# A two-layer encoder step on one core: when loaded operands are cast, and in which order a lone block's seven products run

## The chip, the cores and the metric

The kernel runs on one core of a Trainium2 chip. The metric is the device time of one execution in microseconds (us), the median of several runs. TensorE (PE) does the matrix products, VectorE (DVE), ScalarE (ACT) and GpSimd (POOL) the rest; SyncE (SP) issues most of the loads and stores. Each engine takes its instructions in the order in which they stand in its queue.

## The reference

Two residual layers work on 1088 rows of 1024 features (1024 prompt frames, 64 frames of a running stream). Layer 0 mixes by a state-space scan, layer 1 by attention over a band of chunks; each is followed by a feed-forward part (FFN). The change lies in the FFN's first product, `u @ w_in`, and in the handing over to the second:

```python
def swiglu(u, w_in, w_out):
    g, up = jnp.split(u @ w_in, 2, axis=-1)
    return (jax.nn.silu(g) * up) @ w_out

def reference(...):
    for layer in range(DEPTH):
        ...                         # mixer or attention, with its norms
        xp = xp + rmsnorm(swiglu(rmsnorm(xp, nw[2]), ffn_w_in[layer], ffn_w_out[layer]), nw[3])
        xs = xs + rmsnorm(swiglu(rmsnorm(xs, nw[2]), ffn_w_in[layer], ffn_w_out[layer]), nw[3])
```

The hidden width is 2816: 22 tiles of 128 columns for the gate g and 22 for up.

## The kernel before

**Split operands.** Every float32 operand is used as a sum of two parts that TensorE takes at full speed: a high part, cast on ACT (L365 for weights, L1182 for activations, L1682 and L1710 for what is loaded for the second product), and a low part, the difference to it (L366, L1183, L1683, L1711, on DVE, and on POOL for one weight half). A product of two such operands is three matrix products: hi by hi, hi by lo, lo by hi (L1477 to L1479).

**Seven products for eight.** The rows are cut in halves, and so are the 1024 features. For a gate tile and its up tile together, the two by two blocks are multiplied with seven products P1 to P7 instead of eight, each of 12 matrix products (4 blocks of features by 3). The row operands a11, a21, ..., and their sums s1 to s4, are made once a layer by `op_build` for two row blocks, b=0 (256 columns a product) and b=1 (288). The weight operands are made for every pair of tiles t by `Weights.pair`: "ta" and "tb" are each two differences (L323, L324, on POOL, and L341, L342, on DVE), "r0" is a plain half and "b22" a quarter with its own small buffer `half`. Each is split as above.

**One pair of tiles, `run_pair`.** P1, P6 and P7 add up in one PSUM bank, A: after each, ACT copies the partial sum out (L1490, into p1, u2, u3), and the next may only then add on. P5 and P3 share a bank B where a pair runs for both row blocks. DVE adds the other products to the copies (L1492, L1495, L1498, L1500, L1506), ACT takes Silu (L1493, L1501), DVE multiplies gate and up (L1503, L1508). The order of the products is a list:

```python
PRODS = [
    (P1, "r0", 0, 0), (P2, "r0", 512, 2), (P6, "ta", 0, 1), (P5, "tb", 0, 3),
    (P7, "ta", 512, 5), (P4, "tb", 512, 6), (P3, "b22", 0, 4),
]
```

A pair runs for both row blocks in turn at each product, so that b=0's product lies between b=1's product and the copy of it. Some pairs have no such partner. `RUN` lists the pairs of a layer: in layer 0 t=5 to 21 for both blocks, and then t=0 to 4 for b=1 alone (for b=0 these five tiles are done earlier, without the seven products, by `plain_pairs`); in layer 1 t=5, then t=4 alone, then 6 to 21, then 0 to 3 alone. The first pair of each layer (t=5) is `apart`: all seven products of b=0, then all of b=1, because the splits of b=1 are not made yet. "Lone" below means a pair of b=1 alone.

**Loaders.** The gated results go to DRAM and come back as operands of the second product W2. From the end of t=21 a loader runs beside the lone pairs (`loader` in layer 0, `loader7` in layer 1): it loads a tile into a staging buffer `sg` (five of them), ACT casts it, DVE takes the low part. In layer 1 DVE also forms sums of the results for W2 (`Hidden.form`, L1396) and SP stores them.

**What sets the order.** PE's order is that of the program, with other tasks woven in by a planner (`Stream`) that yields at given times. On ACT, DVE, POOL and SP a scheduler places each instruction by priority (`HIP` for a pair's results, `LDP` for the loaders) and by when its operands are expected.

## Time and profile before

| | |
|---|---|
| median of 3 runs | 3064.5 us (3063.54 to 3070.5) |
| profiled execution | 3060.02 us, of it 3058.1 us span and 1.9 us around it |
| PE, busy | 2949.2 us, 96% of the span |
| DVE | 2228.4 us, 73% |
| ACT | 1478.1 us, 48% |
| POOL | 677.7 us, 22% |
| mean granted clock of PE | 0.988 of full speed |

Times in the rows below are counted from the start of the span. Layer 0's first products with seven instead of eight run from about 940 to 1374 us, the lone pairs from 1312 on; layer 1's from about 2370 to 2806 us, the lone pairs from 2752 on. In a row of the timeline the first two numbers are start and length in us, and the brackets give the idle time of the engine before it and the instruction that ended it. A "waits" row reads: who waited for whom, total us, how often, the longest.

### The profile page before, as it was taken

What the parts mean: (1) busy time and instruction counts of PE and PEld (TensorE: products, weight loads), DVE (VectorE), ACT (ScalarE), POOL (GpSimd) and SP (SyncE); (2) the same over time, 40 slices, a digit from 0 to 9 for tenths busy, and PEclk for the clock granted to TensorE, in tenths of its full rate; (3) what the DMA queues carried; (4) which work ended last, traced back from release to release, by engine and by line L of the source; (5) the groups of instructions that cost most, each with busy time, mean ns of one, the idle gap of its engine ahead of it and who ended that gap; (6) DMA issues with size and microseconds to landing.
All of it is one profiled execution on the core that took longest, in us unless ns stands there. A gap on an engine that the chain in (4) does not pass through costs nothing. (4 is left out here: it accounts for less than half of the span.)

```text
span 3058.1 us, 58284 instructions
## 1 busy us (share of the span) xinstructions
PE 2949.2 (96%) x22017; PEld 2883.2 (94%) x22017; DVE 2228.4 (73%) x4869; ACT 1478.1 (48%) x2834; POOL 677.7 (22%) x809
## 2 busy tenths in 40 slices
PE   8999999999999999989999999999899999999998
PEld 8899999999999999989999898999899999999998
DVE  8988888885878666683666777777668766667567
ACT  6655656554444333353444655555544433344552
POOL 1333333421342221220222000000053221211011
PEclk9999999999999999999999999999999999999999
DMA  3333333335443544445654212222344333235665
GB/s 118 115 91 105 93 102 96 102 111 166 153 138 109 158 133 149 158 146 170 209 177 146 82 62 87 62 62 76 116 140 132 106 108 117 92 120 178 184 193 185
DMA packets 244842, 385.69 MB, mean 126 GB/s; under 512 B 25584, under 2 KB 197168, under 8 KB 244560
## 3 DMA queue, kind: packets, MB, share of 16 engines
q1 hardware_dynamic: 244496, 381.89, 39.8%
q8 instruction: 173, 2.83, 0.4%
q14 instruction: 109, 0.89, 0.1%
q0 software_dynamic: 64, 0.07, 0.0%
HBM read 293.54 MB, written 83.86 MB: 123 GB/s over the span
## 5 line engine op out<-in xcount | busy, mean ns | idle before, releaser
L486 PE MATMUL mm<-r,hl 128*128 128x384 f32 (+2 forms) x1632 | 548.3, 336 | 6.8 <-ACT r L2161 6.0
L488 PE MATMUL mm<-r,hl 128*128 128x384 f32 (+2 forms) x1632 | 530.2, 325 | 3.6 <-DVE hl L378 2.7
L487 PE MATMUL mm<-r,hl 128*128 128x384 f32 (+2 forms) x1632 | 529.4, 324 | 0.7 <-DVE r L2162 0.7
L366 DVE TENSOR_TENSOR hl<-raw,hl 128x1024 fp32r<-128x1024 f32 (+1 forms) x245 | 288.0, 1176 | 200.5 <-ACT hl L365 193.8
L1478 PE MATMUL px<-r,hl 128*128 128x288 f32 (+1 forms) x1192 | 351.4, 295 | 0.0
L365 ACT CAST hl<-raw 128x1024 fp32r<-128x1024 f32 (+1 forms) x245 | 240.8, 983 | 191.1 <-PE po L1854 51.0
L1477 PE MATMUL px<-r,hl 128*128 128x288 f32 x1056 | 312.9, 296 | 13.8 <-ACT u L1490 8.3
L486 PEld LDWEIGHTS mm<-r,hl 128*128 128x128 f32 x1632 | 311.1, 191 | 8.7 <-ACT r L2161 6.2
L488 PEld LDWEIGHTS mm<-r,hl 128*128 128x128 f32 x1632 | 310.3, 190 | 5.3 <-DVE hl L378 4.2
L487 PEld LDWEIGHTS mm<-r,hl 128*128 128x128 f32 x1632 | 311.1, 191 | 1.4 <-DVE r L2162 1.0
L1479 PE MATMUL px<-r,hl 128*128 128x288 f32 x1056 | 311.8, 295 | 0.0
L512 POOL TENSOR_TENSOR ssum<-ssum,sq 128x256 f32<-128x256 f32 (+3 forms) x146 | 157.6, 1082 | 526.2 <-ACT sq L511 512.3
L1477 PE MATMUL px<-rx,hl 128*128 128x256 f32 x816 | 231.0, 283 | 9.6 <-ACT p L1490 9.6
L1479 PE MATMUL px<-rx,hl 128*128 128x256 f32 x816 | 229.9, 282 | 0.5 <-DVE hl L366 0.5
L1478 PEld LDWEIGHTS px<-r,hl 128*128 128x128 f32 x1192 | 225.8, 189 | 0.0
L1477 PEld LDWEIGHTS px<-r,hl 128*128 128x128 f32 x1056 | 199.7, 189 | 15.7 <-ACT u L1490 9.7
L1479 PEld LDWEIGHTS px<-r,hl 128*128 128x128 f32 x1056 | 199.4, 189 | 0.0
L1478 PE MATMUL px<-rx,hl 128*128 128x256 f32 x680 | 191.1, 281 | 0.0
L323 POOL TENSOR_TENSOR tt<-raw 128x512 f32<-128x512 f32 x44 | 61.5, 1398 | 584.1 <-DVE hl L366 513.3
L1490 ACT COPY u<-px 128x288 f32<-128x288 f32 (+1 forms) x156 | 60.1, 386 | 224.0 <-PE px L1479 209.2
L1477 PEld LDWEIGHTS px<-rx,hl 128*128 128x128 f32 x816 | 156.3, 192 | 10.3 <-ACT p L1490 10.3
L1479 PEld LDWEIGHTS px<-rx,hl 128*128 128x128 f32 x816 | 156.2, 191 | 0.8 <-DVE hl L366 0.8
(420 smaller groups left out, 8595.0 us busy)
## 6 DMA issues: line engine op xcount, KB each, us to landing
raw<-in_w_f_dram SPq DMA_DIRECT2D x156, 512.0 KB, 3.8
raw<-in_w_in_dram SPq DMA_DIRECT2D x40, 512.0 KB, 3.5
raw<-in_w_so_dram SPq DMA_DIRECT2D x32, 512.0 KB, 3.8
raw<-in_w_f_dram SPq DMA_DIRECT2D x33, 384.0 KB, 3.2
dm<-acd SPq DMA_DIRECT2D x64, 192.0 KB, 3.6
sg<-hop SPq DMA_DIRECT2D x77, 144.0 KB, 3.0
sg<-hop SPq DMA_DIRECT2D x83, 128.0 KB, 3.1
sg<-in_w_f_dram SPq DMA_DIRECT2D x48, 192.0 KB, 3.1
```

What stands on the lines that cost most here:

```text
L323: g(ta[:, 512:], b22, b12, op=ALU.subtract)
L365: self.nc.scalar.copy(h, v)
L366: (eng or self.eng or self.nc.vector).tensor_tensor(lo, v, h, op=ALU.subtract)
L486: PE.matmul(ps[:, :n], h_, xh, start=(first and i == 0), stop=False)
L487: PE.matmul(ps[:, :n], h_, xl, start=False, stop=False)
L488: PE.matmul(ps[:, :n], l_, xh, start=False, stop=(last and i == nk - 1))
L512: (eng or G).tensor_tensor(ssum[:, :n], ssum[:, :n], q[:, :n], op=ALU.add)
L1477: PE.matmul(ps, wh, ah[:, k, :], start=(k == 0 and not on), stop=False, skip_group_check=on)
L1478: PE.matmul(ps, wh, al[:, k, :], start=False, stop=False, skip_group_check=on)
L1479: PE.matmul(ps, wl, ah[:, k, :], start=False, stop=(k == 3), skip_group_check=on)
L1490: A.copy(x[nm_], ps)
```

## The change

Six edits, all in what surrounds the first product:

1. Pairs that are lone or apart use another order of products, `SINGLE`: P1, P3, P6, P2, P7, P5, P4. Here P3 gets its own bank (C), and P2 and P4 another (D); u2 takes C after P6 and B after P5, c22 is made after P5, and both multiplies come with P4.
2. In `op_build` for b=1 the sums come in the order s3, s2, s4, s1, and the splits in the order in which `SINGLE` uses them.
3. For the pair after the first and for lone pairs ("dve") the differences of L323 and L324 and the low part of b22 are made on VectorE, not on GpSimd.
4. The cast of b22 is gated in every pair: a one-column copy on POOL into its buffer reads the last pair's `ta`, so that the cast cannot come before that is made.
5. The loaders' casts are no longer issued with their loads. `late_cast` holds them back until two later loads are issued, and gates each by a one-column copy on POOL from `hid.gate`, the result that ACT copied out last. The loads get a planned pause (`LGAP`: 1.5 us in layer 0, 0.5 in layer 1).
6. `form` writes s2 into a tile of its own ("ssum", three buffers), and its groups are gated by `hid.gate`.

```diff
+LAHEAD, LGAP = 2, (1.5, 0.5)
...
     def pair(self, it):
-            g = self.nc.gpsimd.tensor_tensor
+            g = (self.nc.vector if "dve" in it else self.nc.gpsimd).tensor_tensor
...
-            self.part(it, "b22", self.half, b22, self.nc.gpsimd)
+            self.part(it, "b22", self.half, b22, self.nc.vector if "dve" in it else self.nc.gpsimd, self.last)
...
+                if key == "ta":
+                    self.last = it["ta"][0]
...
     def part(self, it, key, ring, v, eng=None, gate=None):
         h, lo = t[:, 0, :n], t[:, 1, :n]
+        if gate is not None:
+            self.nc.gpsimd.tensor_copy(h[:, 0:1], gate[:, 0:1])
...
+SINGLE = [
+    (P1, "r0", 0, 0), (P3, "b22", 0, 4), (P6, "ta", 0, 1), (P2, "r0", 512, 2),
+    (P7, "ta", 512, 5), (P5, "tb", 0, 3), (P4, "tb", 512, 6),
+]
...
     def ffn_plan(layer):
+            if i == 1 or len(bs) == 1:
+                it["dve"] = 1
...
     def form(self, b, t_, x, F, S):
-                    ("s3", q[0], a11, a21, ALU.subtract), ("s2", q[0], a22, q[0], ALU.subtract),
-                    ("s4", S, a12, q[0], ALU.subtract), ("s1", F, a21, a22, ALU.add),
+                    ("s3", q[0], a11, a21, ALU.subtract), ("s2", q[1], a22, q[0], ALU.subtract),
+                    ("s4", S, a12, q[1], ALU.subtract), ("s1", F, a21, a22, ALU.add),
...
     def run_pair(t_, pr, bs, ends, ops, hid, px, tmp, apart=False):
+        one = apart or len(bs) == 1
-        for (p_, key, c0, i), b in [(x, b) for b in bs for x in PRODS] if apart else [(x, b) for x in PRODS for b in bs]:
+        for (p_, key, c0, i), b in [(x, b) for b in bs for x in SINGLE] if one else [(x, b) for x in PRODS for b in bs]:
...
+            bank = {P1: "A", P6: "A", P7: "A", P5: "B", P3: "C" if one else "B", P2: "D", P4: "D"}[p_]
...
                 if p_ in (P1, P6, P7):
-                    A.copy(x[nm_], ps)
+                    hid.gate = t_new({P1: "p1", P6: "u2", P7: "u3"}[p_])
+                    A.copy(hid.gate, ps)
...
+                if one:
+                    if p_ == P6:
+                        add("u2", "C")
+                    elif p_ == P5:
+                        t_new("c22")
+                        add("c22", "B", "u3")
+                        add("u2", "B")
+                    elif p_ == P4:
+                        times(0, "p1", "u2", x["c22"])
...
+            def late_cast(left):
+                while len(wait) > left:
+                    at, key, h_, l_, t_, more = wait.pop(0)
+                    if phase[0] < 2 and left:
+                        G.tensor_copy(h_[:, 0:1], hid.gate[:, 0:1])
+                    with tc.high_priority(LDP):
+                        A.copy(h_, t_)
+                        V.tensor_tensor(l_, t_, h_, op=ALU.subtract)
+                    at[key] = h_, l_, *more
...
             def loader():
                         with tc.high_priority(LDP):
                             nc.sync.dma_start(t_, hd[:, k, o:o + n])
-                            A.copy(h_, t_)
-                            V.tensor_tensor(l_, t_, h_, op=ALU.subtract)
-                        hl[s][k] = h_, l_, c, cells
+                        wait.append((hl[s], k, rr(c[0][0]), rr(c[1][0]), t_, (c, cells)))
+                        if phase[0] < 2:
+                            yield 0, LGAP[layer]
+                        late_cast(LAHEAD if phase[0] < 2 else 0)
+                    late_cast(0)
```

`loader7` changes in the same way. In the changed kernel's line numbers L370 is the weights' cast (L365 before), L371 its low part (L366), L1191 the activations' cast (L1182), L1512 the copy of results (L1490), L1515 and L1518 the Silus, L1706 and L1707 the loader's cast and low part, L1704 its gate, L368 the gate of b22.

Three places where the rows move. First ACT at the first pair of layer 0 (t=5, b=0 alone): `half` and `tt` are the weight casts of the next pair's b22 and of this pair's tb, `r<-r` casts row operands of b=1, `p` and `u` are copies of results. Before:

```order
L365 CAST half<-raw 128x512
L365 CAST hl<-tt 128x1024
L1182 CAST r<-r 128x1152
L1490 COPY p_11422<-px 128x256
L1493 ACTIVATE p_11422<-p_11422 128x256
L1182 CAST r<-r 128x1152
L1490 COPY u_11455<-px 128x256
L1182 CAST r<-r 128x1152
```

and now:

```order
L370 CAST half<-raw 128x512
L370 CAST hl<-tt 128x1024
L1512 COPY p_11423<-px 128x256
L1512 COPY u_11454<-px 128x256
L1191 CAST r<-r 128x1152
L1515 ACTIVATE p_11423<-p_11423 128x256
L1191 CAST r<-r 128x1152
```

The copies of p and of u2 move ahead of one cast of a row operand and of Silu; the two weight casts stay where they were.

Second, ACT from the end of t=21 to the first lone pair of layer 0 (`rx<-sg` and `r<-sg` are the loader's casts, p and the next u the results of t=0). Before:

```order
L1501 ACTIVATE u_15562<-u_15562 128x256
L1682 CAST r<-sg 128x384
L365 CAST hl<-tt 128x1024
L1501 ACTIVATE u_15578<-u_15578 128x288
L1682 CAST rx<-sg 128x384 x2
L1682 CAST r<-sg 128x384
L365 CAST half<-raw 128x512
L1682 CAST r<-sg 128x384
L1490 COPY p_15757<-px 128x288
L365 CAST hl<-raw 128x1024
L1493 ACTIVATE p_15757<-p_15757 128x288
L1490 COPY u_15789<-px 128x288
```

and now:

```order
L1518 ACTIVATE u_15583<-u_15583 128x256
L370 CAST hl<-tt 128x1024
L1518 ACTIVATE u_15599<-u_15599 128x288
L370 CAST half<-raw 128x512
L1512 COPY p_15703<-px 128x288
L1512 COPY u_15733<-px 128x288
L370 CAST hl<-raw 128x1024
L1515 ACTIVATE p_15703<-p_15703 128x288
L1512 COPY u_15769<-px 128x288
L370 CAST hl<-tt 128x1024
L1706 CAST rx<-sg 128x384 x2
L370 CAST hl<-tt 128x1024
```

All loader casts have left the place before P1 of t=0; the first two now stand behind that pair's copy of u3, and the copy of u2 stands ahead of Silu.

Third, POOL from the last steady pair of layer 1 into the lone ones (with the numbers of the buffers; `half` is b22, `tt` the differences; p1, u2 and u3 of t=0 are 32013, 32067 and 32129). Before:

```order
L366 TENSOR_TENSOR half_31910<-raw_31834,half_31910 128x512
L323 TENSOR_TENSOR tt_32131<-raw_32100 128x512
L366 TENSOR_TENSOR half_32150<-raw_32100,half_32150 128x512
L324 TENSOR_TENSOR tt_32132<-raw_32100,raw_31913 128x512
L323 TENSOR_TENSOR tt_32259<-raw_32234 128x512
L366 TENSOR_TENSOR half_32279<-raw_32234,half_32279 128x512
L324 TENSOR_TENSOR tt_32260<-raw_32234,raw_32153 128x512
```

and now:

```order
L368 COPY half_31758<-hl_31686 128x1
L368 COPY half_31991<-hl_31917 128x1
L1704 CAST rx_32004<-p1_32013 128x1 x2
L1704 CAST rx_32031<-u2_32067 128x1 x2
L1704 CAST rx_32058<-u2_32067 128x1 x2
L1704 CAST rx_32089<-u3_32129 128x1 x2
L1704 CAST rx_32106<-u3_32129 128x1
L368 COPY half_32211<-hl_32143 128x1
L1704 CAST rx_32136<-u3_32129 128x1 x2
L1704 CAST rx_32156<-u3_32129 128x1
L1704 CAST rx_32185<-p1_32236 128x1 x2
L1704 CAST rx_32227<-p1_32236 128x1 x2
```

In the lone pairs POOL has no differences and no low halves any more, but one-column copies that read the results. Six of them read u3 of t=0, which VectorE later adds to.

More of the change, by code (lines that the diff above doesn't have):

```diff
@@ L245, in __init__ @@
         self.hx, self.used = Ring(None, "hx", 0, hl.shape, hl.dtype), []
-        self.lent, self.own = [], []
+        self.lent, self.own, self.last = [], [], None
     def plan(self, *items):
@@ L1197, in op_build @@
         if ops.b:
-            for x in sums:
+            for x in (sums[0], sums[1], sums[3], sums[2]):
                 if x[0] not in L:
@@ L1466, in t_new, with times, add @@
             def t_new(tag):
-                return tmp.tile([P, n], F32, tag=f"{tag}{b if len(bs) > 1 else t_ % 2}", name=tag)
+                x[tag] = tmp.tile([P, n], F32, tag=f"{tag}{b if len(bs) > 1 else t_ % 2}", name=tag)
+                return x[tag]
+            def times(row, p, q, other):
+                d = hid.out(b, t_, row, other)
+                V.tensor_tensor(d, x[p], x[q], op=ALU.mult)
+                hid.row(b, t_, row, d)
+            def add(d, bank, y=None):
+                V.tensor_tensor(x[d], x[bank][:, :n], x[y or d], op=ALU.add)
             st.wait_for(lambda: i in ops[b].hl)
             ah, al = ops[b].hl[i]
-            on = p_ in (P6, P7) or (p_ == P3 and len(bs) > 1)
-            if p_ in (P1, P5):
-                x["A" if p_ == P1 else "B"] = px.tile([P, 512], F32, tag="mm", name="px")
-            ps = (x["B" if p_ in (P5, P3) else "A"] if on or p_ in (P1, P5) else mm("px"))[:, :n]
+            bank = {P1: "A", P6: "A", P7: "A", P5: "B", P3: "C" if one else "B", P2: "D", P4: "D"}[p_]
+            on = p_ in (P6, P7) or (p_ == P3 and not one)
+            if not on:
+                x[bank] = px.tile([P, 512], F32, tag="mm", name="px") if bank in "AB" else mm("px")
+            ps = x[bank][:, :n]
             for k in range(4):
@@ L1499, in run_pair @@
                 elif p_ == P4:
-                    V.tensor_tensor(x["u3"], ps, x["u3"], op=ALU.add)
+                    add("u3", "D")
                     A.activation(x["u3"], x["u3"], AF.Silu)
-                    d = hid.out(b, t_, 1, x["u3"])
-                    V.tensor_tensor(d, x["u3"], x["c22"], op=ALU.mult)
-                    hid.row(b, t_, 1, d)
-                elif p_ == P3:
-                    V.tensor_tensor(x["u2"], ps, x["u2"], op=ALU.add)
-                    d = hid.out(b, t_, 0, x["c22"])
-                    V.tensor_tensor(d, x["p1"], x["u2"], op=ALU.mult)
-                    hid.row(b, t_, 0, d)
+                    times(1, "u3", "c22", x["u3"])
@@ new lines, in run_pair @@
+                if one:
[7 more added lines that the diff above has]
+                        times(0, "p1", "u2", x["c22"])
+                else:
+                    if p_ == P7:
+                        t_new("c22")
+                        add("c22", "B", "u3")
+                    elif p_ == P3:
+                        add("u2", "B")
+                        times(0, "p1", "u2", x["c22"])
@@ L1510, in run_pair @@
             for _ in range((len(hid.late) > 0) + (len(hid.late) > 4 and len(bs) == 1) if p_ != P1 or b == bs[-1] else 0):
-                hid.late.pop(0)(x[{P1: "p1", P2: "p1", P6: "u2", P5: "u2", P7: "u3", P4: "u3", P3: "u2"}[p_]])
-            if p_ == P3:
+                hid.late.pop(0)(hid.gate)
+            if p_ == (P4 if one else P3):
                 hid.sums(b, t_, x["c22"], x["u3"])
@@ L1703, in loader7 @@
                     ):
[L1704 removed]
+                        ready = lambda: (b, k) in hid.ok and sh.room((b, k, 0), (b, k, 1))
+                        if not ready():
+                            late_cast(0)
+                        yield 0, 0, ready
                         h_, l_ = (rr(sh.get((b, k, part))) for part in range(2))
@@ L1709, in loader7 @@
                             nc.sync.dma_start(t_, hop[:, OPN[p_], k, b * 256:b * 256 + n])
-                            A.copy(h_, t_)
-                            V.tensor_tensor(l_, t_, h_, op=ALU.subtract)
-                        hl[p_, b, k] = h_, l_, sh
+                        wait.append((hl, (p_, b, k), h_, l_, t_, (sh,)))
+                        if phase[0] < 2:
+                            yield 0, LGAP[layer]
+                        late_cast(LAHEAD if phase[0] < 2 else 0)
+                    late_cast(0)
             done7 = set()
@@ L1829, in back @@
                 W.tt.bufs = W.half.bufs = 0
+                W.last = None
             phase[0] = 2
```

33 lines of the change are left out of this document (14 added, 19 removed).

## The prediction

> **What bounds the kernel now.** I read the page first, then the waits of PE, then the granted clock by window, and last the timelines of ACT, DVE and POOL at the places where PE stood.
>
> ```profile
> PE 2949.2 (96%) x22017; PEld 2883.2 (94%) x22017; DVE 2228.4 (73%) x4869; ACT 1478.1 (48%) x2834; POOL 677.7 (22%) x809
> ```
>
> PE is the bound. The change neither adds nor drops a matrix product, so it can only win back time in which PE waits inside the first products, or lose more there. The view of waits (total, times, longest) gives that time:
>
> ```profile
> PE px L1477 <- ACT p L1490: 15.2, 5, 4.9
> PE px L1477 <- ACT u L1490: 8.3, 6, 1.8
> ...
> PE px L1477 <- DVE c L1498: 2.1, 2, 1.3
> ...
> PE px L1479 <- DVE hl L366: 0.5, 1, 0.5
> ```
>
> That is 15.2 + 8.3 + 2.1 + 0.5 = 26.1 us. The timeline of PE says where (start, length, and in brackets the idle time before):
>
> ```profile
> 950.41 0.58 PE L1477 MATMUL px<-rx,hl 128*128 128x256 f32 x1 [4.94 <-ACT p L1490]
> 1307.34 0.41 PE L1477 MATMUL px<-r,half 128*128 128x288 f32 x1 [1.32 <-DVE c L1498]
> 1315.43 0.61 PE L1477 MATMUL px<-r,hl 128*128 128x288 f32 x1 [3.03 <-ACT p L1490]
> 1333.08 0.40 PE L1477 MATMUL px<-r,hl 128*128 128x288 f32 x1 [1.77 <-ACT u L1490]
> 2378.45 0.38 PE L1477 MATMUL px<-rx,hl 128*128 128x256 f32 x1 [3.58 <-ACT p L1490]
> 2408.30 0.40 PE L1477 MATMUL px<-r,hl 128*128 128x288 f32 x1 [1.18 <-ACT u L1490]
> 2420.44 0.39 PE L1477 MATMUL px<-rx,hl 128*128 128x256 f32 x1 [1.13 <-ACT p L1490]
> 2755.50 0.61 PE L1477 MATMUL px<-r,hl 128*128 128x288 f32 x1 [2.48 <-ACT p L1490]
> 2773.34 0.40 PE L1477 MATMUL px<-r,hl 128*128 128x288 f32 x1 [1.82 <-ACT u L1490]
> 2786.32 0.40 PE L1477 MATMUL px<-r,hl 128*128 128x288 f32 x1 [1.52 <-ACT u L1490]
> ```
>
> Behind four of these gaps the clock falls to half, for 6.9, 3.5, 6.9 and 3.5 us; in the first stretch of lone pairs, with gaps up to 1.77 us, it stays at 1.00 (columns: window, its length, busy time and count of PE, PEld, DVE, ACT, POOL, the granted clock, the DMA share, GB/s):
>
> ```profile
> 949.60:956.50 6.90, 6.09 (x28) 6.09 (x29) 6.90 (x6) 3.54 (x6) 3.63 (x2) 0.51 0.21 61
> 1314.80:1318.30 3.50, 2.87 (x12) 2.87 (x13) 3.50 (x6) 1.96 (x4) 3.50 (x2) 0.51 0.87 238
> 2379.80:2386.70 6.90, 6.37 (x31) 6.08 (x30) 6.90 (x7) 3.18 (x6) 1.57 (x2) 0.51 0.23 76
> 2755.30:2758.80 3.50, 3.30 (x14) 3.31 (x15) 3.40 (x8) 1.17 (x3) 0.78 (x1) 0.52 0.49 120
> ...
> 1328.00:1374.00 46.00, 42.25 (x314) 41.54 (x314) 39.10 (x53) 24.16 (x42) 13.41 (x8) 1.00 0.40 121
> ```
>
> Half of 6.9 + 3.5 + 6.9 + 3.5 = 20.8 us is lost: 10.2 us with the clocks shown. The 3.5 us cases have 0.6 and 0.2 us of idle PE in their window; in the first half of the 6.9 us cases stand 0.8 and some 0.5. So what the change can reach is 26.1 + 10.2 = 36.3 us, and about 0.1 us more for each of the 14 restarts (the first product after a gap lasts 0.40 instead of 0.30).
>
> **The change, place by place.** I replayed the changed order on each engine against the durations below. A place's gain is its loss now less what the replay leaves.
>
> *The first pair of layer 0, all products of b=0 alone; loss 4.94 + 0.74 (the other wait for c) + 3.4 of clock = 9.1 us.*
>
> ```profile
> 947.47 0.62 ACT L365 CAST half<-raw 128x512 fp32r<-128x512 f32 x1 [6.02 <-DMA raw<-in_w_f_dram]
> 948.00 1.04 ACT L365 CAST hl<-tt 128x1024 fp32r<-128x1024 f32 x1
> 948.94 1.15 ACT L1182 CAST r<-r 128x1152 fp32r<-128x1152 f32 x1
> 950.00 0.36 ACT L1490 COPY p<-px 128x256 f32<-128x256 f32 x1
> ```
>
> P6 cannot add into bank A before ACT has copied P1. Of the three casts ahead of that copy, only the last (from 948.94 to 950.00) moves behind it; the half cast that waits for a weight load, and the cast of tb, still stand ahead. So P6 starts 1.0 us sooner, and by then P3 has run in its own bank C, so P5 no longer waits for c. The gap stays near 4 us, so the clock will fall. P6 then starts at 949.4, ahead of the half clock's start at 949.6 in the window above, and no wait is left in its first 3.4 us, so I count one such stretch instead of two as in the 3.5 us cases: 1.7 us saved. Gain 1.0 + 0.7 + 1.7 = 3.4 (bounds 1.0, the copy alone, and 5.1 with both windows gone).
>
> *The first pair of layer 1; loss 3.58 + 0.53 + 3.4 = 7.5.* The same cast moves (gain 1.0), tb's low half moves up (0.5 less 0.4 that the new order waits for a split), and the second half-clock stretch goes as above (1.7): 2.8 (1.0 to 5.1).
>
> *Tile pair 21 of layer 0; loss 1.3.* P4 waits for DVE's c22, whose u3 copy stands behind three loader casts on ACT. These casts now come later: gain 1.3 (0 to 1.3).
>
> *The pairs 4 and 6 of layer 1; loss 1.18 + 1.13 = 2.3.* In pair 4 the b22 half is VectorE's and the copy goes ahead of Silu: 1.2. In pair 6 the copy of p still waits for a multiply behind a sum that waits for GpSimd: 0. Gain 1.2 (0 to 2.3).
>
> *The five lone pairs of layer 0; loss 3.03 + 1.77 + 1.1 + 0.9 for the next two + 1.7 of clock = 8.5.* (The 1.1 + 0.9 are two gaps that the row for u counts: 8.3 less the four shown is 2.0.) Two causes stand in the trace. The copy of p waits behind loader casts and a half cast:
>
> ```profile
> 1313.50 0.61 ACT L365 CAST half<-raw 128x512 fp32r<-128x512 f32 x1
> 1314.57 0.51 ACT L1682 CAST r<-sg 128x384 fp32r<-128x384 f32 x1 [0.45 <-DMA sg<-hscr]
> 1314.98 0.39 ACT L1490 COPY p<-px 128x288 f32<-128x288 f32 x1
> ```
>
> and the copy of u2 waits behind Silu, Silu behind DVE's add to p, and that add behind a sum and a multiply that are slow because they run beside GpSimd:
>
> ```profile
> 1332.30 0.44 ACT L1493 ACTIVATE p<-p 128x288 f32<-128x288 f32 x1 [3.06 <-DVE p L1492]
> 1332.65 0.38 ACT L1490 COPY u<-px 128x288 f32<-128x288 f32 x1
> ```
>
> ```profile
> 1328.03 1.78 DVE L341 TENSOR_TENSOR tt<-tt,raw 128x512 f32<-128x512 f32 x1 [1.41 <-POOL tt L323]
> 1329.73 1.57 DVE L1508 TENSOR_TENSOR c<-p,u 128x288 f32<-128x288 f32 x1
> 1331.22 0.68 DVE L342 TENSOR_TENSOR tt<-raw,tt 128x512 f32<-128x512 f32 x1
> 1331.82 0.44 DVE L1492 TENSOR_TENSOR p<-px,p 128x288 f32<-128x288 f32 x1
> 1332.19 1.21 DVE L366 TENSOR_TENSOR hl<-raw,hl 128x1024 fp32r<-128x1024 f32 x1
> 1333.32 0.44 DVE L1495 TENSOR_TENSOR u<-px,u 128x288 f32<-128x288 f32 x1
> ```
>
> ```profile
> 1327.95 1.31 POOL L366 TENSOR_TENSOR half<-raw,half 128x512 fp32r<-128x512 f32 x1
> 1329.21 1.77 POOL L324 TENSOR_TENSOR tt<-raw 128x512 f32<-128x512 f32 x1
> ```
>
> With copies of p and u2 ahead of Silu, and with no GpSimd sums in these pairs, both go. What takes their place is load on DVE. From start to start in the rows above a low half takes 1.13 us, a 512-wide operation 0.60, a 288-wide one 0.37. The loader's low half is, in the window of the lone pairs of layer 0 (count, then busy us and mean ns, idle before)
>
> ```profile
> L1683 DVE TENSOR_TENSOR r<-sg,r 128x384 fp32r<-128x384 f32 x10 | 5.3, 551 | 0.1
> ```
>
> 0.55 less the 0.08 by which starts follow sooner than ends: 0.47. A pair in the new order has 3 low halves (3.4), 5 operations of 512 (two differences, two sums, the half; 3.0), 5 adds and 2 multiplies (2.6) and three to four loader halves (16 over five pairs; 1.4 to 1.9): 10.4 to 10.9 us. PE needs 42.25/314 = 0.135 us a product, 84 of them 11.3 us. It fits by 0.4 to 0.9 us, with small waits at single points; I leave 1.0 us over five pairs. Gain 7.5 (0 to 8.5; zero if DVE does not keep up).
>
> *The lone pairs of layer 1 (t=0 to 3); loss 2.48 + 1.82 + 1.52 + 1.7 of clock = 7.5.* The same count over the new order gives DVE 13.1, 11.6 and 11.2 us in the first three pairs and some 6 in the last, so it falls behind by 2.1 us first and catches up last. One new wait stands in the order: the add to u3 of t=0 waits on VectorE for GpSimd's one-column copies that read u3, and these for a loader cast which ACT has behind its copy of u2 for t=1. Bank D is free only after that add, so P2 of t=1 waits 2.2 us in the replay. Whether it costs the clock too is open: 1.82 us above did not, 2.48 did; 2.2 is nearer to 2.48, and I take half of that window's 1.7. Left 2.2 + 0.9 = 3.1; gain 4.4 (0 to 6.5).
>
> The Trainium skill, "TensorE: Matmul & The Clock Gate", Part 1, has the clock fall only after an idle window of about 3.4 us. The row at 2755.50 shows a half clock after 2.48 us, so the measurement decides here; by the page that 0.9 would be nothing, nor would the 1.7 that I leave at the first pair of layer 1, whose gap shrinks to 2.6: the forecast would be 2.6 us lower.
>
> *Costs at nothing.* The one-column copies on POOL, 16 and 14 to 22 loader gates and one for each b22 half, run on an engine with 13.4 busy of 46 us here; that is their cover, and what stands behind them on POOL in steady pairs is only the next half. SP has the same loads with pauses of 1.5 or 0.5 us between them, and the casts run two loads behind. W2's first products need the loader's operands some us after the replay has the last of them; if the cover fails, each cast that is late costs about 0.5 us there (0 to 4). The separate tile for s2 only frees DVE from waiting for a store.
>
> Sum: 3.4 + 2.8 + 1.3 + 1.2 + 7.5 + 4.4 = 20.6, and 1.0 for some ten restarts: 21.6 us. The profiled execution took 3060.0 us (span 3058.1 and 1.9 around it), so 3038.4; the median of the runs is 3064.5, 4.5 above it, so 3042.9: I say 3043.
>
> **The rivals.**
>
> *VectorE is the bound in the lone pairs.* For it: 39.1 busy of 46 us already in the window above, and 10.9 of 11.3 us by my count. Each one-column copy on POOL might also stop a DVE operation. The nearest such row:
>
> ```profile
> L790 POOL COPY craw<-halo x48: 185/188/1763, 39.2 to 631.0; 128x3 f32<-128x3 f32 x48
> ```
>
> 0.19 us at the median, 4 of them a pair 0.8; with 0.2 of handing over each, up to 1.6. Then a pair takes 11.7 to 12.5 us, 0.4 to 1.2 more than PE; at 0.9, five pairs lose 4.5 us and the gain of 7.5 becomes 4; in layer 1 some 18 copies, 5 us, on top of 2.9 behind leave nothing of 4.4. Gain 21.6 − 3.5 − 4.4 − 1 = 12.7: 3052. Against it: the rows for slow DVE operations all lie beside long POOL operations. The Trainium skill, "SBUF — State Buffer", makes the pair of ports that VectorE and GpSimd share an exclusive lock: a VectorE operation with two inputs waits out a GpSimd one. The row at 1329.73, 1.57 us long, ends 0.3 us after the GpSimd row from 1329.21 does, so the trace agrees. It speaks against the gates here as well as for the sums' move.
>
> *The casts are not really held back.* At the first pairs the half cast waits for its load as before, and nothing but the cast at 948.94 moves. If the scheduler's order runs another way on the chip, or the clock drops for two stretches as now, 3.4 and 2.8 fall to 1.0 or less each: gain 17.4, 3047.
>
> *A gated cast holds up the copies behind it (slower).* ACT is in order. A loader cast that waits for POOL's copy, and this for a result, stands on ACT ahead of the next result's copy; if POOL answers late in every lone pair, PE stops at P6 or P7 of all nine. It decides from the point where each stop costs more than (21.6 + 9.2 + 4.1)/9 = 3.9 us, where 4.1 is what the replay leaves there. At the size of the gap at 2755.50 with its clock, 2.48 + 1.7 = 4.2, nine cost 38 us in place of those 4.1: 34 lost, and with 21.6 gained 12 slower: 3077. Against it: the copies gate two loads behind, so mostly the result is long there.
>
> *All of it goes.* If the gaps at the first pairs fall below the clock's limit and no new wait appears: 36.3 + 1.4 = 38: 3027.
>
> **How the numbers follow.** Chances: the forecast 0.60 (alone 3034 to 3050), VectorE 0.14, casts not held back 0.12, slower by gated casts 0.06, all of it 0.08. The range 3027 to 3058 leaves out the slower case and the far end of VectorE's. A measurement of this kernel can tell about 0.3%, 9.2 us, from no change: faster is below 3055.3. The forecast, all of it and casts not held back are faster but for small parts, VectorE for two thirds: 0.84. Within 0.3%: 0.10, mostly VectorE. Slower: 0.06.
>
> **What the changed profile would show.** Right: the wait of px for p falls from 15.2 to some 8 us, 6.5 of it at the two first pairs, the one for u from 8.3 to below 2, the one for c is gone; the clock stays at 1.00 in the lone pairs of layer 0; a wait of some 2 us for VectorE's u3 at P2 of the second lone pair of layer 1. The sums at the lone pairs take 0.68 on DVE. Wrong: gaps for VectorE in each lone pair, DVE busy for over 97% there; a gap at the first W2 product; or gaps for p and u that are as long as before.

## The result, and the profile after

The changed kernel takes 3049.1 us (median of four runs, 3048.59 to 3051.33) against 3065.6 us before: a ratio of 0.9945, interval 0.9928 to 0.9963, so 16.5 us faster. The forecast was 3043, with 3027 to 3058 as its range. Direction and range hold; the gain is 5 us smaller than the 21.6 forecast.

PE is the bound as before, with as many matrix products; VectorE's busy time fell from 2228.4 to 2193.8 us although it took work over from GpSimd. The first row of the page after:

```profile
PE 2949.8 (97%) x22017; PEld 2883.7 (95%) x22017; DVE 2193.8 (72%) x4906; ACT 1475.2 (48%) x2834; POOL 660.6 (22%) x852
```

The waits of PE in the first products (total, times, longest):

```profile
PE px L1500 <- ACT p L1512: 12.5, 7, 4.4
...
PE px L1500 <- DVE u L1489: 2.0, 2, 1.6
```

26.1 us of idle time became 12.5 + 2.0 = 14.5 and a few tenths. The waits for u by ACT and for c are gone; those for p are not 8 us, as the prediction said, but 12.5. The timeline of PE shows where (idle time in brackets):

```profile
948.55 0.38 PE L1500 MATMUL px<-rx,hl 128*128 128x256 f32 x1 [3.77 <-ACT p L1512]
1341.43 0.40 PE L1500 MATMUL px<-r,hl 128*128 128x288 f32 x1 [0.68 <-ACT p L1512]
1353.55 0.40 PE L1500 MATMUL px<-r,hl 128*128 128x288 f32 x1 [0.67 <-ACT p L1512]
2370.19 0.38 PE L1500 MATMUL px<-rx,hl 128*128 128x256 f32 x1 [1.76 <-ACT p L1512]
2411.72 0.58 PE L1500 MATMUL px<-rx,hl 128*128 128x256 f32 x1 [4.39 <-ACT p L1512]
2758.80 0.40 PE L1500 MATMUL px<-r,hl 128*128 128x288 f32 x1 [0.93 <-ACT p L1512]
2762.31 0.40 PE L1500 MATMUL px<-r,hl 128*128 128x288 f32 x1 [1.65 <-DVE u L1489]
```

The waits at the first pairs (948.55 and 2370.19) got shorter, from 4.94 and 3.58 us, and the lone pairs lost most of theirs. The longest is at a place that had 1.13 us before: pair 6 of layer 1, right behind the lone pair 4. The windows (columns as in the prediction) show what the clock did: half clock for 3.5 us at the first pair of layer 0 instead of 6.9, none in the lone pairs of layer 0 (from 1303.92 to 1361.65 now), and a new stretch of 7 us around the wait of 4.39:

```profile
949.50:953.00 3.50, 3.50 (x20) 3.50 (x19) 3.50 (x6) 1.43 (x2) 0.00 (x0) 0.51 0.29 82
953.00:956.50 3.50, 3.50 (x31) 3.50 (x31) 3.40 (x5) 2.86 (x5) 0.00 (x0) 1.00 0.17 68
1303.92:1361.65 57.73, 56.38 (x423) 55.92 (x422) 49.04 (x84) 32.53 (x60) 9.92 (x19) 1.00 0.52 161
...
2410.30:2414.00 3.70, 2.28 (x10) 2.28 (x11) 3.63 (x9) 1.64 (x3) 0.59 (x1) 0.52 0.50 157
2414.00:2417.50 3.50, 3.50 (x18) 3.50 (x17) 1.43 (x2) 0.81 (x3) 0.00 (x0) 0.53 0.78 240
```

To compare places across kernels I use their *loss*: from the start of a place's first matrix product to the start of the first one behind the place, less 1.372 us for each of its products P1 to P7 of 256 columns and 1.594 us for each of 288. These are what a product takes at full clock with no wait; a steady pair, which has no wait, comes out at 0.18 us. Idle time, half clock and restarts are all in it.

| us of loss | before | after | gain forecast | gain found |
|---|---|---|---|---|
| first pair, layer 0 | 9.1 | 5.8 | 3.4 | 3.3 |
| pair 21, layer 0 | 1.8 | 0.2 | 1.3 | 1.6 |
| lone pairs, layer 0 | 9.1 | 1.9 | 7.5 | 7.2 |
| first pair, layer 1 | 7.8 | 3.1 | 2.8 | 4.7 |
| pairs 4 and 6, layer 1 | 3.1 | 8.0 | 1.2 | -4.9 |
| lone pairs, layer 1 | 8.1 | 3.1 | 4.4 | 4.9 |
| steady pairs | 5.3 | 5.8 | 0 | -0.5 |
| sum | 44.3 | 28.0 | 20.6 and 1.0 for restarts | 16.3 |

The sum of 16.3, from one profiled execution of each kernel, is near what the medians show (16.5). The span of these two executions fell by only 11.3 us, because 5.8 were lost in the stage between the two first products; the last section has that.

### The profile page after: what moved, and what is told of

The parts are those of the page before. It is cut to its first block, busy times and chain, and to the rows that moved or that the text cites. A ratio compares the mean times of both kernels' runs of the same rounds, so it can differ in the third digit from the quotient of the medians.

```text
span 3046.8 us, 58392 instructions
## 1 busy us (share of the span) xinstructions
PE 2949.8 (97%) x22017; PEld 2883.7 (95%) x22017; DVE 2193.8 (72%) x4906; ACT 1475.2 (48%) x2834; POOL 660.6 (22%) x852
## 5 line engine op out<-in xcount | busy, mean ns | idle before, releaser
L371 DVE TENSOR_TENSOR hl<-raw,hl 128x1024 fp32r<-128x1024 f32 (+1 forms) x245 | 287.2, 1174 | 204.4 <-ACT hl L370 203.0
L370 ACT CAST hl<-raw 128x1024 fp32r<-128x1024 f32 (+1 forms) x245 | 240.8, 984 | 189.8 <-PE po L1903 48.2
L1489 DVE TENSOR_TENSOR c<-px,u 128x256 f32<-128x256 f32 (+1 forms) x78 | 34.5, 442 | 198.1 <-ACT u L1512 198.1
L1512 ACT COPY u<-px 128x288 f32<-128x288 f32 (+1 forms) x156 | 60.4, 388 | 224.3 <-PE px L1502 224.1
```

Source lines behind the costliest of these rows:

```text
L370: self.nc.scalar.copy(h, v)
L371: (eng or self.eng or self.nc.vector).tensor_tensor(lo, v, h, op=ALU.subtract)
```

## The experiments

Each row gives the loss in us of its own profiled execution, then the median time and the ratio to the kernel before, run on the same chip. "First" are the two first pairs, "lone" the lone pairs of layer 0 and of layer 1, "4, 6" those two pairs of layer 1.

| kernel | first, L0 | first, L1 | lone, L0 | lone, L1 | 4, 6 | sum | median us | ratio (interval) |
|---|---|---|---|---|---|---|---|---|
| before | 9.1 | 7.8 | 9.1 | 8.1 | 1.4, 1.6 | 44.3 | 3065.6 | 1 |
| changed | 5.8 | 3.1 | 1.9 | 3.1 | 0.6, 7.4 | 28.0 | 3049.1 | 0.9945 (0.9928 to 0.9963) |
| e1, old order | 6.8 | 5.5 | 1.9 | 9.1 | 1.9, 0.2 | 30.8 | 3048.8 | 0.9943 (0.9929 to 0.9958) |
| e2, sums on GpSimd | 7.6 | 6.6 | 10.2 | 8.9 | 0.1, 7.6 | 47.0 | 3068.4 | 1.0011 (1.0000 to 1.0021) |
| e3, casts with loads | 6.1 | 3.2 | 1.5 | 0.7 | 0.6, 7.2 | 25.5 | 3045.0 | 0.9931 (0.9916 to 0.9946) |
| e4, P2 second | 9.7 | 7.1 | 5.8 | 11.2 | 1.6, 2.5 | 43.2 | 3061.9 | 0.9983 (0.9974 to 0.9992) |
| e5, sums alone | 6.9 | 7.1 | 2.8 | 0.8 | 1.5, 1.5 | 26.1 | 3049.5 | 0.9945 (0.9925 to 0.9965) |
| e6, no b22 gate | 5.7 | 5.0 | 1.9 | 2.9 | 0.1, 7.3 | 28.8 | 3048.3 | 0.9948 (0.9931 to 0.9964) |
| e7, own buffers | 5.9 | 3.1 | 1.8 | 2.5 | 0.6, 3.4 | 23.5 | 3045.1 | 0.9935 (0.9920 to 0.9950) |
| e8, pair 4 old order | 5.9 | 3.2 | 2.0 | 5.8 | 0.6, 2.7 | 26.0 | 3045.2 | 0.9937 (0.9922 to 0.9951) |
| e9, e3 and e7 | 6.0 | 3.2 | 1.0 | 1.5 | 0.7, 2.1 | 20.5 | 3041.3 | 0.9923 (0.9911 to 0.9936) |
| e10, order in first pairs only | 5.6 | 3.3 | 2.0 | 0.5 | 0.6, 2.1 | 20.1 | 3040.9 | 0.9920 (0.9906 to 0.9933) |
| e11, changed again | 5.8 | 3.2 | 1.9 | 2.8 | 0.6, 7.7 | 28.0 | 3048.4 | 0.9949 (0.9936 to 0.9961) |

The last kernel repeats the changed one: its places lose the same to 0.4 us, so differences of a microsecond between rows of the table mean something, while single times scatter by several. One caution holds for all rows: a stretch of half clock more or less moves a place by 1.7 or 3.4 us, and the last section shows that waits of the same length do not always bring one. The experiments take edits away or add them singly only in part: edit 2 was undone only together with edit 1, and edit 6 was not looked at by itself.

**What makes pair 6 lose?** The chain in the changed kernel, by engine. DVE:

```profile
2400.00 1.22 DVE L371 TENSOR_TENSOR hl<-raw,hl 128x1024 fp32r<-128x1024 f32 x1
...
2408.03 1.74 DVE L342 TENSOR_TENSOR tt<-tt,raw 128x512 f32<-128x512 f32 x1 [2.38 <-POOL tt L324]
2409.69 1.51 DVE L1485 TENSOR_TENSOR c<-p,u 128x288 f32<-128x288 f32 x1
```

POOL, and ACT:

```profile
2406.71 1.29 POOL L324 TENSOR_TENSOR tt<-raw 128x512 f32<-128x512 f32 x1 [3.60 <-DMA raw<-in_w_f_dram]
```

```profile
2411.29 0.37 ACT L1512 COPY p<-px 128x256 f32<-128x256 f32 x1 [3.75 <-DVE c L1485]
```

The low half of pair 6's r0 (2400.00) is the last reader of a raw weight buffer, so only after it can the next load go; it lands at 2406.7, POOL makes the difference, DVE the sum, and behind that sum on DVE stands pair 4's last multiply, which reads pair 4's p1. The copy of p of pair 6 goes into that same buffer, so ACT waits, and so does P6. Before, the same chain ran: the low half at 2408.19, POOL at 2414.97, the multiply at 2418.35, the copy at 2420.02.

```profile
2408.19 1.22 DVE L366 TENSOR_TENSOR hl<-raw,hl 128x1024 fp32r<-128x1024 f32 x1
...
2418.35 1.55 DVE L1508 TENSOR_TENSOR c<-p,u 128x288 f32<-128x288 f32 x1
```

Counted from the start of pair 6 (2413.18 before, 2401.14 after), the low half came 5.0 us ahead before and 1.1 us ahead now, 3.9 us later. Theory A: in the new order P2 is fourth, and P2 is the last user of r0, so the buffer for the next r0 comes free two products later. Theory B: the sums that VectorE now makes are late. The cast of pair 6's r0, before and after, speaks for theory A:

```profile
2404.00 1.05 ACT L365 CAST hl<-raw 128x1024 fp32r<-128x1024 f32 x1 [1.25 <-PE px L1479]
```

```profile
2395.97 1.05 ACT L370 CAST hl<-raw 128x1024 fp32r<-128x1024 f32 x1 [1.25 <-PE px L1502]
```

It waits for PE in both kernels. From the start of pair 4 (2400.58 before, 2389.35 after) it comes after 3.4 us, when the second product has ended, and now after 6.6 us, when the fourth has.

*e1_old_order*: lone and first pairs run `PRODS` again.

```diff
-        for (p_, key, c0, i), b in [(x, b) for b in bs for x in SINGLE] if one else [(x, b) for x in PRODS for b in bs]:
+        for (p_, key, c0, i), b in [(x, b) for b in bs for x in PRODS] if apart else [(x, b) for x in PRODS for b in bs]:
...
-            for nm_ in ("a11", "s4", "s2", "a12", "s3", "s1", "a22"):
+            for nm_ in OPI:
...
```

> The new order of products and its banks are undone (lone and first pairs run P1, P2, P6, P5, P7, P4, P3 again, with the old order of the row sums and splits); the other edits stay. Loss below means the time of a place's products beyond 1.372 us each (256 columns) or 1.594 us (288). Theory A, the order of products carries the first pairs and also makes the new loss at pair 6 of layer 1 (P2 stands fourth, so r0's buffer, the next weight load and its sums come two products, 3.2 us, later): first pair of layer 0 from 5.8 to about 9, of layer 1 from 3.1 to about 7.5, pair 6 from 7.4 to about 1.6, lone pairs of layer 0 from 1.9 to some 4; in all some 5 us slower than the changed kernel. Theory B, pair 6 loses because VectorE makes the differences of the pair ahead and is late: pair 6 keeps over 6.

Pair 6 falls from 7.4 to 0.2 us: theory A. But the total stays: the first pairs lose 3.3 us more, the lone pairs of layer 0 stay at 1.9 (I had expected 4), and those of layer 1 go to 9.1, with one wait of 6 us at the second:

```profile
2764.27 0.61 PE L1500 MATMUL px<-r,half 128*128 128x288 f32 x1 [5.99 <-DVE p L1489]
```

```profile
2763.76 0.46 DVE L1489 TENSOR_TENSOR p<-px,p 128x288 f32<-128x288 f32 x1
```

The add to p stands on DVE behind low halves of loader casts, sums and differences; VectorE has no pause over 0.2 us between 2749.5 and 2764.

*e8_pair4_old_order*: only pair 4 of layer 1 runs the old order.

```diff
-        one = apart or len(bs) == 1
+        lone = len(bs) == 1
+        one = (apart or lone) and not (lone and t_ == 4 and hasattr(hid, "form"))
...
```

> Only the lone pair 4 of layer 1 goes back to the old order of products (P2 second); all else as changed. Theory A: r0 is free two products sooner, the next weight load 3 us sooner, pair 6's loss falls from 7.4 to below 1.5 as with the old order throughout (0.2), pair 4's rises from 0.6 to about 1.9; some 5 us faster than the changed kernel. Rival: pair 6 suffers from the first pair's new order as well: over 4 us stay.

The low half of r0 comes sooner again, and POOL's difference with it:

```profile
2397.07 1.21 DVE L371 TENSOR_TENSOR hl<-raw,hl 128x1024 fp32r<-128x1024 f32 x1
```

```profile
2403.93 1.56 POOL L324 TENSOR_TENSOR tt<-raw 128x512 f32<-128x512 f32 x1 [7.76 <-DMA raw<-in_w_f_dram]
```

From the start of pair 6 (2400.45) POOL's difference starts 3.5 us later, against 5.6 in the changed kernel. Pair 6 loses 2.7 instead of 7.4: more than the 1.5 expected, but the mechanism holds. Of the 4.7 us, 2.7 went again in the lone pairs of layer 1 (3.1 to 5.8), which I had not foreseen. There a wait of 1.76 us was followed by 6.8 us of half clock, worth 3.4 us, where the changed kernel, with a wait of 1.65, had none:

```profile
2754.24 0.40 PE L1501 MATMUL px<-r,hl 128*128 128x288 f32 x1 [1.76 <-ACT p L1513]
```

```profile
2754.90:2761.80 6.90, 5.92 (x25) 5.57 (x25) 5.32 (x12) 1.72 (x4) 1.33 (x8) 0.51 0.55 162
```

*e7_own_buffers*: pair 4's p1 and u2 go to staging buffers, so that the copy of p need not wait for the multiply.

```diff
-                x[tag] = tmp.tile([P, n], F32, tag=f"{tag}{b if len(bs) > 1 else t_ % 2}", name=tag)
+                x[tag] = stage[0]()[:, :n] if t_ == 4 and len(bs) == 1 and tag in ("p1", "u2") and hasattr(hid, "form") else tmp.tile([P, n], F32, tag=f"{tag}{b if len(bs) > 1 else t_ % 2}", name=tag)
```

> The lone pair 4 of layer 1 writes its p1 and u2 into staging buffers of their own, so that the copy of p of pair 6 for b=0 need not wait for the multiply of pair 4, which stands on VectorE behind a sum that waits for GpSimd's difference and so for a weight load; order and all else as changed. Theory A (late weight load, handed on through the multiply and the shared buffer): the wait of 4.4 us at P6 falls to 0 to 1 us, pair 6's loss from 7.4 to 0.5 to 3 (ta itself, from the same late load, is for the pair after); about 5 us faster than the changed kernel. Rival: another wait stands right behind (the sum itself or u2): over 5 us stay.

```profile
2409.25 0.39 PE L1500 MATMUL px<-rx,hl 128*128 128x256 f32 x1 [1.31 <-ACT p L1512]
```

The wait falls from 4.39 to 1.31 us and takes the half clock with it; pair 6 loses 3.4, since the late sums hold up the next copy too. Late load and shared buffer are both links of the chain: cutting either gives back 3.9 or 4.7 us.

*e4_p2_second*: P2 second in the new order, the rest as changed.

```diff
-    (P1, "r0", 0, 0), (P3, "b22", 0, 4), (P6, "ta", 0, 1), (P2, "r0", 512, 2),
-    (P7, "ta", 512, 5), (P5, "tb", 0, 3), (P4, "tb", 512, 6),
+    (P1, "r0", 0, 0), (P2, "r0", 512, 2), (P3, "b22", 0, 4), (P6, "ta", 0, 1),
+    (P7, "ta", 512, 5), (P5, "tb", 0, 3), (P4, "tb", 512, 6),
...
```

> One thing moves: P2 is second in the new order (P1, P2, P3, P6, P7, P5, P4), and the splits of b=1 follow. Theory A (P2 in fourth place frees r0 late): pair 6 of layer 1 from 7.4 to below 2 us of loss; and since P2 now lies between P1 and P6, the first pairs fall by 1.4 us each or more (5.8 to 4.4 or, with the half clock gone, 2.7; 3.1 to 1.8); the second lone pair of layer 1 loses its wait for a late weight load too (3.1 to about 1). Some 8 us faster than the changed kernel. Theory B: pair 6 keeps over 5.

Pair 6 falls to 2.5, as theory A says, but the rest was misjudged: this order puts P7 right behind P6, both add into bank A, and so every pair waits for ACT's copy of u2 between them. The waits of PE in this kernel:

```profile
PE px L1500 <- ACT u L1512: 14.0, 14, 2.7
```

14 waits, one for each first or lone pair and block. In this kernel a product that adds to another needs at least one product between them. The second lone pair of layer 1 also got worse, not better: it loses 8.2 us, with a wait of 4.8 us for an add on VectorE and 6.8 us of half clock.

**Which edit carries the lone pairs?** *e2_sums_gpsimd* takes the flag away that moves the differences and b22's low half to VectorE.

```diff
-            if i == 1 or len(bs) == 1:
-                it["dve"] = 1
```

> The differences and the low half of b22 of lone pairs go back to GpSimd; the other edits stay. Theory A, VectorE's operations are slow beside GpSimd's and that makes results late in lone pairs: lone pairs of layer 0 from 1.9 to 4 or 5 us of loss, those of layer 1 from 3.1 to about 5; pair 6 of layer 1 unchanged at 7. Rival, the new order of products has enough room and this edit brings nothing: lone pairs within 0.7 us of the changed kernel. Theory B (see the run with the old order): pair 6 falls below 3.

Nothing is left of the gain (3068.4 us). The lone pairs lose 10.2 and 8.9, more than before the change, and pair 6 stays at 7.6, which refutes theory B. What the flag does is seen in VectorE's own times, grouped by shape over the lone pairs of layer 0. Before, beside GpSimd's sums:

```profile
L341 DVE TENSOR_TENSOR tt<-tt,raw 128x512 f32<-128x512 f32 x4 | 6.4, 1609 | 1.4 <-POOL tt L323 1.4
L1508 DVE TENSOR_TENSOR c<-p,u 128x288 f32<-128x288 f32 x5 | 4.5, 897 | 0.0
```

the changed kernel:

```profile
L342 DVE TENSOR_TENSOR tt<-tt,raw 128x512 f32<-128x512 f32 x4 | 2.7, 684 | 0.0
...
L1485 DVE TENSOR_TENSOR c<-p,u 128x288 f32<-128x288 f32 x5 | 2.3, 453 | 0.0
```

and without the flag:

```profile
L342 DVE TENSOR_TENSOR tt<-tt,raw 128x512 f32<-128x512 f32 x3 | 4.2, 1416 | 1.6 <-POOL tt L324 1.6
L1483 DVE TENSOR_TENSOR c<-p,u 128x288 f32<-128x288 f32 x4 | 4.0, 1005 | 0.0
```

On the mean a sum takes 684 instead of 1609 ns and a multiply 453 instead of 897 when GpSimd has no 512-wide operations in the pair. So the three operations more in a pair cost VectorE less than it got back: over the five lone pairs it is busy for 49.04 us (in the window from 1303.92 above), and was for 56 before:

```profile
1309.04:1373.96 64.92, 58.14 (x422) 57.20 (x421) 56.00 (x80) 34.59 (x61) 22.20 (x12) 0.97 0.44 136
```

Two things are not separated by these runs. GpSimd itself is slow at this work: a difference takes it 1.3 us or more, VectorE alone 0.68, and the raw buffer that it reads can take the next weight load only after it. And in e2 the gates add a loss of their own, since POOL's one-column copies now stand behind its differences, the gated casts wait for them on ACT, and a copy of u stands behind the casts:

```profile
1356.78 0.93 ACT L1704 CAST rx<-sg 128x384 fp32r<-128x384 f32 x2 [4.08 <-POOL rx L1702]
1357.61 0.39 ACT L1510 COPY u<-px 128x288 f32<-128x288 f32 x1
```

PE waits 1.84 us for that copy. So e2 shows more than the worth of the sums, and the next run is the cleaner one.

*e5_sums_alone*: the kernel before with that one edit.

```diff
-            g = self.nc.gpsimd.tensor_tensor
+            g = (self.nc.vector if "dve" in it else self.nc.gpsimd).tensor_tensor
...
+            if i == 1 or len(bs) == 1:
+                it["dve"] = 1
```

> The kernel before with one edit of the change alone: the differences and the low half of b22 of lone pairs (and of the pair after the first) on VectorE. After the run without this edit came out with no gain at all, theory C: this edit carries the lone pairs by itself. Loss at the lone pairs of layer 0 from 9.1 to about 2, of layer 1 from 8.1 to about 2, first pairs 9.1 and 7.8 to some 7 and 6, pair 6 of layer 1 stays at 1.6: about 15 us faster than before, as much as the whole change. Rival, the edit works only with the new order of products or with held-back casts: lone pairs of layer 0 over 5, and under 7 us faster than before.

It is worth as much as the whole change: 3049.5 us, a ratio of 0.9945 in both cases. (Its profiled execution, 3039.2 us, is the fastest of its four, so the places and the ratio count here, not that time.) The sums alone bring the lone pairs to 2.8 and 0.8 and lose nothing at pair 6. All other edits together add 1.1 at the first pair of layer 0, 4.0 at that of layer 1 and 0.9 each at the lone pairs of layer 0 and at pair 4, and take 5.9 back at pair 6 and 2.3 at the lone pairs of layer 1.

This run also tells what moved the cast of a row operand at the first pairs, which I had read as part of the new order. With the sums alone the copy of p follows tb's cast, which ends at 948.26, as in the changed kernel (e5, layer 0):

```profile
948.17 0.36 ACT L1493 COPY p<-px 128x256 f32<-128x256 f32 x1
```

With the new order but the sums on GpSimd the cast still stands ahead of the copy (e2):

```profile
950.38 1.15 ACT L1191 CAST r<-r 128x1152 fp32r<-128x1152 f32 x1
951.43 0.36 ACT L1510 COPY p<-px 128x256 f32<-128x256 f32 x1
```

P6 waits 4.00 us in e5, 4.60 in e2, 4.94 before and 3.77 in the changed kernel. Why the scheduler places the cast later then is not shown.

**Do held-back casts help?** *e3_casts_with_loads*:

```diff
-                        wait.append((hl[s], k, rr(c[0][0]), rr(c[1][0]), t_, (c, cells)))
-                        if phase[0] < 2:
-                            yield 0, LGAP[layer]
-                        late_cast(LAHEAD if phase[0] < 2 else 0)
-                    late_cast(0)
+                            h_, l_ = rr(c[0][0]), rr(c[1][0])
+                            A.copy(h_, t_)
+                            V.tensor_tensor(l_, t_, h_, op=ALU.subtract)
+                        hl[s][k] = h_, l_, c, cells
...
```

> The loaders' casts are issued with their loads again, without gates and pauses; the other edits stay. Theory A, casts ahead of copies on ScalarE made the waits at tile pair 21 and the first lone pairs: pair 21 from 0.2 back to 1.8 us of loss, the first lone pair of layer 0 from 0 to 3 or 4.5, that of layer 1 up by 2; some 6 us slower in all. Rival, the new order alone gives the copies room: under 1.5 us in all places together.

The opposite of the expectation: without holding back the places lose 2.5 us less. The median is 4 us lower (3045.0 against 3049.1), but the intervals of the two ratios overlap. The lone pairs of layer 1 lose 0.7 instead of 3.1. Those of layer 0 lose 1.5 instead of 1.9: the first of them 1.4 more, where 3 or 4.5 had been expected, the last two 0.9 each less. Pair 21 stays at 0.2, and it is at 0.2 in every variant. In e5, which has only edit 3, and in e3 two loader casts still stand ahead of its copy of u3; e2 has all edits but edit 3. So more than one edit can take its wait away, holding the casts back is not needed for it, and what did it in the changed kernel is not settled by these runs.

*e6_no_b22_gate* leaves the gate of b22 out.

```diff
-            self.part(it, "b22", self.half, b22, self.nc.vector if "dve" in it else self.nc.gpsimd, self.last)
+            self.part(it, "b22", self.half, b22, self.nc.vector if "dve" in it else self.nc.gpsimd)
```

> The gate of b22's cast is left out, all else as changed. Theory: the gate does not decide, since at the first pairs the half cast stands ahead of the copy of p with or without it: first pairs 5.8 and 3.1 as they are within 1 us, lone pairs within 1.5 us, pair 6 of layer 1 at 7; total within 3 us of the changed kernel. Rival: the gate is what keeps half casts from standing ahead of copies in the lone pairs: 3 us or more lost there.

The time is the same within the runs' scatter (3048.3). The first pair of layer 1 loses 1.9 more, which is over the 1 us that I had allowed: P6 waits 3.06 us there, and 3.4 us at half clock, worth 1.7, follow. Pair 4 loses 0.5 less.

**What beats both?** *e9_buffers_plain_casts* is e3 with the edit of e7. *e10_order_first_only* is e3 with the new order in the first pairs only:

```diff
-        one = apart or len(bs) == 1
+        lone = len(bs) == 1
+        one = (apart or lone) and not lone
...
```

> Two of the findings together on the changed kernel: the loaders' casts go with their loads, and pair 4 of layer 1 has buffers of its own for p1 and u2. If the places add up, the loss of all places is 25.5 (casts with loads) less 3.9 (pair 6 with own buffers): some 21.5 us against 28.0 in the changed kernel, 3043 us or a little less. Rival, the gains overlap or the order shifts elsewhere: over 25.

> The changed kernel with the loaders' casts with their loads, and the new order of products in the two first pairs only; lone pairs run the old order. Theory: the sums on VectorE serve the lone pairs, the new order is worth its place only where b=0 runs alone first: first pairs 5.8 and 3.2 us of loss as in the changed kernel, lone pairs of layer 0 some 1.5 to 2.8, of layer 1 below 1, pairs 4 and 6 1.5 each: places 20 us in all, 3042 us. Rival, the b22 gate with the old order costs the lone pairs of layer 1 (9.1 where the old order met gates and held-back casts): over 5 there.

> The changed kernel itself beside the two others, for a direct comparison: ratio to before 0.994 to 0.996; the loss of its places 28 us as in its first profile, within 1.5.

The places add up: 20.5 and 20.1 us of loss against 28.0. e10 takes 3040.9 us, ratio 0.9920 (0.9906 to 0.9933), against 0.9949 (0.9936 to 0.9961) for the changed kernel beside it: the intervals are apart. It does without held-back casts and with less new code than the change, and its lone pairs of layer 1 lose 0.5 where the old order with held-back casts (e1) lost 9.1.

## Why the prediction was right or wrong

- *PE is the bound, and the change can reach 36.3 us in the first products*: right. The gain in those places is 16.3 us, and the medians, 16.5 us apart, leave nothing to explain from elsewhere.
- *First pair of layer 0, gain 3.4*: found 3.3, with the steps as forecast. The copy of p follows the half cast and tb's cast, the gap shrank by 1.17 to 3.77 us, the wait for c is gone, and 3.4 us of half clock are left instead of 6.8. But the prediction read the cast's move off the rows without asking which edit made it. It was the sums' move to VectorE: e5, without the new order, gains 2.2 of the 3.3 us here. The new order took the wait for c away; e5 and e1, without it, still wait some 0.8 us for c.
- *First pair of layer 1, gain 2.8*: found 4.7. The clock stayed at full speed, so the 1.7 us that I had left for it came on top, and that part was luck: e6 lost it again behind a gap of 3.06 us. The gap itself was 1.76 us here and 2.71 in the repeat (e11), where 2.6 was forecast, and the loss was 3.1 or 3.2 both times.
- *Lone pairs of layer 0, gain 7.5*: found 7.2. The move of GpSimd's sums carried it, as e5 shows. VectorE's operations do get faster by it, as the prediction argued, but how much comes from that and how much from GpSimd's own slowness is not separated. The other half of the argument, copies ahead of Silu and casts held back, did not: e1 has the old order and loses as little, e3 casts with the loads and loses as little, and e5 with neither loses 0.9 more.
- *Pair 21, gain 1.3*: found 1.6. The number came out, but that is no proof of its cause: the wait is gone as well where loader casts still stand ahead of the copy (e3, e5).
- *VectorE busy 10.4 to 10.9 of 11.3 us*: too high. The five lone pairs of layer 0 have 49.04 busy of 57.73, 9.8 of 11.5 in a pair. That rival fell in layer 0. Its price for the one-column copies, with 0.2 us of handing over each, is borne out by no run: in the changed kernel's first products the 24 multiplies of 288 columns with such a copy beside them took 448 ns on the mean, the 6 with nothing beside them 454. In layer 1 VectorE did become the last to arrive, with held-back casts (the changed kernel and e1) and hardly without them (e3, e10).
- *Pair 6 of layer 1, gain 0 ("the copy of p still waits for a multiply behind a sum that waits for GpSimd")*: this step failed, and it is the main error. The chain was named, but I took its length over from the trace of before. I did not ask when the load at its head would start under the new order: r0 is free two products later, its low half comes 3.9 us later, and the wait grew from 1.13 to 4.39 us with 7 us of half clock. With pair 4 that is -4.9 instead of +1.2, 6.1 us in all, more than the whole difference to the forecast; the 1.9 us more than forecast at the first pair of layer 1 hid a part of it.
- *Lone pairs of layer 1, gain 4.4*: found 4.9, and the new wait at P2 of t=1 was there, 1.65 us for 2.2. Its cause was not the one named. GpSimd's last copy that reads u3 before the add ended at 2755.1, far ahead of it (two of the six that read u3 ran only at 2764.13, after the Silu behind the add):

```profile
2753.91 1.20 POOL L1704 CAST rx<-u 128x1 fp32r<-128x1 f32 x1
```

```profile
2757.51 0.69 DVE L324 TENSOR_TENSOR tt<-raw 128x512 f32<-128x512 f32 x1 [1.05 <-DMA raw<-in_w_f_dram]
...
2761.43 0.45 DVE L1707 TENSOR_TENSOR rx<-sg,rx 128x288 fp32r<-128x288 f32 x1
2761.80 0.45 DVE L1489 TENSOR_TENSOR u<-px,u 128x288 f32<-128x288 f32 x1
```

  VectorE waited for a weight load and then worked without a pause through seven operations to the add. It was VectorE's queue, with the difference that the change had put there, and not a wait for GpSimd.
- *The clock*: the gaps of 1.76 and 1.65 us, and 2.71 in the repeat, left it at full speed, so the 1.7 and 0.9 that I had kept for them were not lost. The rule on the Trainium skill's page ("TensorE: Matmul & The Clock Gate", Part 1) gives the same here. Its figure of some 3.4 us of idle still does not fit the gap of 2.48 us before, nor that of 1.76 in e8.
- *A gated cast holds up what is behind it (slower, 0.06)*: not in that size, but the sign was right for layer 1: e3 shows 2.4 us. The way was another there: with held-back casts 21 of the loader's low halves lie in these pairs, 8.5 us of VectorE, in e3 9, and PE waited for VectorE, not for a copy on ACT. The way that the prediction named shows in e2, where GpSimd is busy.
- *W2's first products, 0 to 4 us*: nothing was lost there. PE has no gap at the first W2 products of either layer.

## What to carry to other kernels

When an order of operations changes, follow each buffer to its last reader and ask what load that reader lets go: a product moved by two places moved a weight load by nearly 4 us, four instructions ahead of the wait that it caused. Work on VectorE with two inputs in SBUF should be priced with GpSimd's operations beside it; moving GpSimd's work onto the busier engine made that engine faster here. And when a change has six edits, run them apart: one of them alone was worth as much as all six together.
